# Last down projections of a float32 decoder trunk: loads, high parts, sums and low parts chained in the order of the matmuls; the final gain loaded in four pieces

## The chip, the cores and the metric

The kernel runs on one core of a Trainium2 chip. Its time is the device time of one execution in microseconds; smaller is better. A trace of one profiled execution is read beside it. PE is the matmul engine (PEld its weight loads), DVE the vector engine, ACT the scalar engine, POOL the general-purpose engine, and SP the sequencer that issues nearly all loads.

## What is computed

The reference is a two-layer decoder trunk on 256 tokens of width 2048, all in float32. The first layer has a gated spatial mixer, the second a latent attention; both attend to a memory and end in a gated feed-forward block. The change is in the feed-forward block of the second layer and in the final norm:

```python
def conv_ffn(h, w_up, cw, cb, w_down):
    ...
    gate, val = c[..., :D_FF], c[..., D_FF:]
    return (jax.nn.silu(gate) * val) @ w_down
...
x = x + conv_ffn(rmsnorm(x, g_ffn[l]), w_up[l], conv_w[l], conv_b[l], w_down[l])
return rmsnorm(x, g_final)
```

`w_down` is 5632 x 2048 (44 row blocks of 128).

## The kernel before

**Two parts for each number.** A float32 product is made of three matmuls in the faster type fp32r: every operand is split into a high part (a rounding copy on ACT, tile `whi`) and a low part (the rest, a subtraction on DVE, tile `wlo`), and PE adds high x high, high x low and low x high. So each weight tile of 128x1024 that is loaded (tile `raw` or `gate`) needs one copy on ACT and one subtraction on DVE before PE can use it; the first and third matmul need only `whi`, the second needs `wlo`. There are 4 buffers for `whi`, 5 for `wlo`, 4 for `raw`, 2 for `gate`: a load waits until the subtraction that last read its buffer is done, and a copy into `whi` waits until PE has done with the tile that had the buffer.

**The second layer's feed-forward.** It goes in three parts of 4, 4 and 3 groups of 512 columns (`FF_GROUPS`). In each part PE first makes the hidden values (up projections, L156 to L159, weights through L117 and L118), then the down projection of those columns in two phases, one for each half of 1024 output columns (`down_phase`). A phase walks over blocks `k` of two row blocks each, in an order written out in `FF_FAST`: (0, 1, 2, 5, 3, 6, 7, 4) in the first two parts, with the blocks 2, 3 and 4 "fast"; in the third part (0, 1, 3, 2, 4, 5) with 1 and 2 fast, and then (0, 1, 2, 3, 4, 5) with 1 fast.

A plain block takes its two tiles as they are (`plain_pair`) and costs 24 matmuls of 512 columns, 2 copies and 2 subtractions. A fast block (`fast_pair`) does the 2x2 block product with 7 products in place of 8 (21 matmuls). For that DVE makes four sums of quarter tiles into two tiles `xs` (L720 to L723) from the block's tiles x and y; then y, the two `xs` tiles (L715, L716) and the left half of x (tile `we`, L726, L727) are split. Its products use them in the order y, the second `xs` tile, the first `xs` tile; the product with `we` can stand anywhere. The two tiles of a fast block come into `gate` buffers, except those of the first fast block in a part, which come into `raw`. The same two `gate` buffers hold the up projection's gate values before; the second of them comes free only with the last product "gate times value" (L863, tile `hv`) of the part.

**Who sets the order.** The code is written block after block, but a scheduler that is part of the build orders the instructions of each engine by its own model of their times. It may move a sum, a copy or a load ahead of others that stand before it in the code, and each engine then works strictly in the order that it was given: an instruction that waits holds up all behind it. Only in the last two blocks of the last phase (`late=2`) does the code fix the order for PE, DVE and ACT.

**The end.** `Tokens` collects the results: `between` copies the four extra sums of a phase's fast blocks (tiles `staged`), `combine` folds them into the residual `xt` (six DVE operations, L1353), `evict` adds the four plain sums (L1372) and, in the third part, squares them and multiplies with the final gain `gb` (L1392). `gb` is `g_final` repeated over the 128 partitions, 1 MB as it lands, loaded in one piece at the start of the third part's first phase (L1341).

Of the kernel before, what the change touches and what calls it, by code (L numbers as in the profile page):

```python
# [8 lines left out]
F32 = mybir.dt.float32  # L9
# [3 lines left out]
AF = mybir.ActivationFunctionType  # L13
ALU = mybir.AluOpType
AX = mybir.AxisListType

P = 128
D = 2048
# [55 lines left out]
class Kernel:  # L74
# [235 lines left out]
    def gains(self, names):  # L310
        self.gain_turn(self.gain_load(names, self.nc.sync))
# [352 lines left out]
    def halves(self):  # L664
        tiles = [self.ap.tile([P, NB // 2, 512], F32R, tag=f"xhl{i}", name=self.uid("xhl")) for i in range(2)]
        return [tiles[k // (NB // 2)][:, k % (NB // 2), :] for k in range(NB)]
# [28 lines left out]
                done()  # L695


    def plain_pair(self, raws):
        nc, out = self.nc, []
        for raw in raws:  # L700
            hi, lo = self.split_tile("whi", True), self.split_tile("wlo", True)
            nc.scalar.activation(hi, raw, AF.Copy)
            nc.vector.tensor_tensor(lo, raw, hi.bitcast(F32), ALU.subtract)  # L703
            out.append((hi, lo))
        return out

    def fast_pair(self, raws, pool):
        nc, tt = self.nc, self.nc.vector.tensor_tensor
        left, right = slice(0, 512), slice(512, 1024)
        x, y = raws  # L710
        sums = [self.tmp(pool, [P, 1024], "xs", 2) for _ in range(2)]

        def parts(w):
            hi, lo = self.split_tile("whi", True), self.split_tile("wlo", True)
            nc.scalar.activation(hi, w, AF.Copy)  # L715
            tt(lo, w, hi.bitcast(F32), ALU.subtract)  # L716
            return [(hi[:, c], lo[:, c]) for c in (left, right)]

        t13, t24 = sums
        tt(t13[:, left], x[:, left], x[:, right], ALU.add)  # L720
        tt(t13[:, right], x[:, right], y[:, right], ALU.add)
        tt(t24[:, left], t13[:, left], y[:, right], ALU.add)  # L722
        tt(t24[:, right], t24[:, left], y[:, left], ALU.add)  # L723
        b21, b22 = parts(y)
        one = self.tmp(pool, [P, 1040], "we", 1, F32R)[:, :1024]
        nc.scalar.activation(one[:, left], x[:, left], AF.Copy)  # L726
        tt(one[:, right], x[:, left], one[:, left].bitcast(F32), ALU.subtract)  # L727
        b11 = one[:, left], one[:, right]
        t2, t4 = parts(t24)
        t1, t3 = parts(t13)  # L730
        return b21, b22, t4, t2, t1, t3, b11


    def down_phase(self, dn, col, order, fast, lhs, rhs, pool, fp, between, evict, finish, late=0):
        mm = self.nc.tensor.matmul
        names = ("m1", "m5", "m6", "m7"), ("e00", "e01", "e10", "e11")
        acc = {n: self.psum() for group in names[::-1] for n in group}
        left, right = slice(0, 512), slice(512, 1024)
        todo = {n: 0 for n in acc}
        for k in order:  # L740
            for n in ("m1", "m5", "m6", "m7", "e00", "e01", "e10") if k in fast else names[1]:
                todo[n] += 1 if k in fast else 2
        total = dict(todo)

        def three(n, x, w, out=None, ends=None):
            (xh, xl), (wh, wl) = x, w
# [3 lines left out]
            mm(o, xh, wh, start=start, stop=False)  # L750
            mm(o, xh, wl, start=False, stop=False)  # L751
            mm(o, xl, wh, start=False, stop=stop)  # L752

        def plain(k, ws, tb, half, **kw):
            cols = (left, right)[half]
            for i, (wh, wl) in enumerate(ws):
                three(f"e{tb}{half}", lhs(2 * k + i, tb), (wh[:, cols], wl[:, cols]), **kw)

        kept = []
        last_fast = [k for k in order if k in fast][-1]  # L760
        for n, k in enumerate(order):
            raws = []
            for i in range(2):
                if k in fast and (col or k != fast[0]):
# [3 lines left out]
                self.nc.sync.dma_start(out=raw, in_=dn[(2 * k + i) * P : (2 * k + i + 1) * P, col : col + 1024])  # L768
                raws.append(raw)
            if k in fast:  # L770
                names7 = "e00", "e01", "e10", "m6", "m5", "m7", "m1"
                for name, q, w in zip(names7, (1, 6, 2, 5, 4, 3, 0), self.fast_pair(raws, pool)):
                    three(name, rhs(k, q), w)
                if k == last_fast:
                    between([acc[m] for m in names[0]])
            else:
                ws = self.plain_pair(raws)
                if n < len(order) - late:
                    for tb in range(2):
                        for half in range(2):  # L780
                            plain(k, ws, tb, half)
                else:
                    kept.append((k, ws))
        if not late:
            for tb in range(2):
                for half in range(2):
                    evict(tb, half, acc[f"e{tb}{half}"])
            return
        ET = mybir.EngineType
        with self.tc.manual_schedule(engines={ET.PE, ET.DVE, ET.Activation}):  # L790
            for half in range(2):
                for k, ws in kept:
# [12 lines left out]
            evict(1, 1, e, 0)  # L805
            for i, (wh, wl) in enumerate(ws):
                three("e11", lhs(2 * k + i, 1), (wh[:, 768:], wl[:, 768:]), out=rest[:, 256:], ends=(i == 0, i == 1))
            evict(1, 1, rest, 1)
            finish(1)


    def ffn(self, l, after=None, to_tokens=None, tokens=None):
        nc, t = self.nc, self.t
# [4 lines left out]
        with self.tc.tile_pool(name=self.uid("ff"), bufs=1) as fp:  # L818
            g0 = 0
            for part, ng in enumerate(FF_GROUPS):  # L820
                h = self.ap.tile([P, NB * 512], F32R, tag="big", name=self.uid("h"))
                last = part == len(FF_GROUPS) - 1
                phases = FF_FAST[ng] if tokens is not None else (((), ()), ((), ()))
                fast = phases[0][0]
                if tokens is None:
                    plain = {k: h[:, 1024 * k : 1024 * (k + 1)] for k in range(2 * ng)}
                else:
                    parts7, o = {}, 0
                    for k in fast:
                        n = 896 if k in phases[1][0] else 1024  # L830
# [63 lines left out]
                dn = down[g0 * 512 : (g0 + ng) * 512]  # L894
                g0 += ng
                if tokens is not None:

                    rhs = lambda k, q: tuple(parts7[k][:, i, q * P : (q + 1) * P] for i in range(2))

                    def lhs(k, tb):  # L900
                        if k // 2 in parts7:
                            return rhs(k // 2, ((0, 7), (1, 2))[k % 2][tb])
                        x = block(k)
                        return x[:, tb * P : (tb + 1) * P], x[:, S + tb * P : S + (tb + 1) * P]

                    for ph in range(2):
                        tokens.begin(ph, last)
                        self.down_phase(
                            dn, 1024 * ph, phases[ph][1], phases[ph][0], lhs, rhs, tokens.pool, fp, tokens.between, tokens.evict, tokens.finish, late=2 if last and ph else 0
                        )  # L910
                    continue
                for j in range(4):
# [387 lines left out]
class Tokens:  # L1300
# [32 lines left out]
    def begin(self, ph, last):  # L1333
        k = self.k
        self.ph, self.last = ph, last
        if ph == 0:
            self.staged = k.ap.tile([P, 2, 4, 512], F32, tag="xT", name=k.uid("staged"))
            if last:
                self.gb = k.ap.tile([P, 2 * D], F32, tag="xhl0", name="gb")[:, :D]
                g = k.t["g_final"].rearrange("(o d) -> o d", o=1).to_broadcast([P, D])  # L1340
                self.nc.sync.dma_start(out=self.gb, in_=g)  # L1341

    def between(self, accs):
        for i, acc in enumerate(accs):
# [98 lines left out]
```

## Time and profile before

| what | value |
|---|---|
| device time, 3 runs | median 2054.26 us (2053.43 to 2055.97) |
| profiled execution: its own time, its span | 2056.95 us, 2055.2 us |
| busy share of the span: PE, DVE, ACT, POOL | 99%, 73%, 54%, 7% |
| mean granted clock of PE | 0.998 |
| bytes read from HBM | 387.88 MB, 190 GB/s over the span |
| the chain that ended last | PE 88%, DVE 6%, DMA 4%, issue 1%, ACT 1% |
| loads of `w_ffn_down` into `raw`, into `gate` | 152 and 24 of 512 KB, median 4.6 and 4.8 us from issue to landing |

The span is the stretch from the first to the last instruction; the device time of that execution is 1.75 us longer. A row of a timeline gives the start and the length of an instruction, and in brackets how long its engine stood idle before it and what ended the idle time. Matmuls overlap, so the start of one to the start of the next is what one costs. Lines like L716 are lines of the kernel before.

### The profile page before, as it was taken

What the parts mean: (1) busy time and instruction counts of PE and PEld (TensorE: products, weight loads), DVE (VectorE), ACT (ScalarE), POOL (GpSimd) and SP (SyncE); (2) the same over time, 40 slices, a digit from 0 to 9 for tenths busy, and PEclk for the clock granted to TensorE, in tenths of its full rate; (3) what the DMA queues carried; (4) which work ended last, traced back from release to release, by engine and by line L of the source; (5) the groups of instructions that cost most, each with busy time, mean ns of one, the idle gap of its engine ahead of it and who ended that gap; (6) DMA issues with size and microseconds to landing.
All of it is one profiled execution on the core that took longest, in us unless ns stands there. A gap on an engine that the chain in (4) does not pass through costs nothing.

```text
span 2055.2 us, 39936 instructions
## 1 busy us (share of the span) xinstructions
PE 2034.6 (99%) x16229; PEld 1962.0 (95%) x16229; DVE 1503.4 (73%) x2280; ACT 1114.7 (54%) x1611; POOL 142.0 (7%) x200
## 2 busy tenths in 40 slices
PE   9999999999999999999999999999999999999997
PEld 8889999999999999999999999999988999889976
DVE  6866767767656776567788787777787777878777
ACT  6754744555435554345545675455555555555554
POOL 0000013000000000000042242300000000000000
PEclk9999999999999999999999999999999999999999
DMA  8776566666666666666665535668755766557653
GB/s 251 230 218 181 165 194 194 193 193 193 195 194 194 195 195 195 194 192 192 193 195 183 172 119 165 195 193 228 216 190 179 204 193 206 187 176 205 195 192 135
DMA packets 233821, 394.68 MB, mean 192 GB/s; under 512 B 53854, under 2 KB 61348, under 8 KB 233508
## 3 DMA queue, kind: packets, MB, share of 16 engines
q1 hardware_dynamic: 233444, 391.58, 63.5%
q8 instruction: 127, 2.08, 0.4%
q14 instruction: 58, 0.48, 0.1%
q10 hardware_dynamic: 192, 0.54, 0.1%
HBM read 387.88 MB, written 2.10 MB: 190 GB/s over the span
## 4 chain that ended last, share of the span: by engine, by line
PE 88%; DVE 6%; DMA 4%; issue 1%; ACT 1%; SPq 0%; DVEq 0%; ACTq 0%
PE ps L156 25%; PE ps L157 25%; PE ps L159 25%; DMA gate<-in_w_ffn_down 3%; PE ps L188 2%; PE ps L189 2%; PE ps L190 2%; DVE wlo L703 2%; DMA raw<-in_w_ffn_down 1%; DVE wlo L716 1%; PE ps L523 1%; PE ps L751 1%; PE ps L752 1%; PE ps L750 1%; DVE xs L722 0%
## 5 line engine op out<-in xcount | busy, mean ns | idle before, releaser
L118 DVE TENSOR_TENSOR wlo<-raw,whi 128x1024 fp32r<-128x1024 f32 x572 | 710.1, 1245 | 383.4 <-ACT whi L117 378.7
L117 ACT ACTIVATE whi<-raw 128x1024 fp32r<-128x1024 f32 x572 | 607.1, 1062 | 685.8 <-PE ps L157 583.3
L156 PE MATMUL ps<-xhl,whi 128*128 128x256 f32 x3264 | 762.9, 277 | 0.0
L157 PE MATMUL ps<-xhl,whi 128*128 128x256 f32 x3264 | 761.3, 276 | 0.0
L156 PEld LDWEIGHTS ps<-xhl,whi 128*128 128x128 f32 x3264 | 612.9, 188 | 0.4
L157 PEld LDWEIGHTS ps<-xhl,whi 128*128 128x128 f32 x3264 | 612.7, 188 | 0.4
L159 PE MATMUL ps<-xhl,wlo 128*128 128x256 f32 x3264 | 436.6, 276 | 0.0
L159 PEld LDWEIGHTS ps<-xhl,wlo 128*128 128x128 f32 x3264 | 400.4, 188 | 0.0
L156 PE MATMUL ps<-h,whi 128*128 128x256 f32 x704 | 163.6, 276 | 0.0
L157 PE MATMUL ps<-h,whi 128*128 128x256 f32 x704 | 163.6, 276 | 0.0
L157 PEld LDWEIGHTS ps<-h,whi 128*128 128x128 f32 x704 | 131.9, 188 | 0.0
L156 PEld LDWEIGHTS ps<-h,whi 128*128 128x128 f32 x704 | 131.9, 188 | 0.0
L156 PE MATMUL ps<-mainhl,whi 128*128 128x256 f32 x512 | 119.6, 277 | 0.0
L157 PE MATMUL ps<-mainhl,whi 128*128 128x256 f32 x512 | 119.4, 276 | 0.0
L844 ACT ACTIVATE c<-a,cT 128x256 f32<-128x256 f32 x176 | 99.4, 590 | 10.7 <-DVE a L236 10.6
L157 PEld LDWEIGHTS ps<-mainhl,whi 128*128 128x128 f32 x512 | 96.0, 188 | 0.0
L156 PEld LDWEIGHTS ps<-mainhl,whi 128*128 128x128 f32 x512 | 95.9, 188 | 0.0
L159 PE MATMUL ps<-h,wlo 128*128 128x256 f32 x704 | 94.1, 276 | 0.0
L751 PE MATMUL ps<-wlo,h 128*128 128x512 f32 (+1 forms) x228 | 90.1, 395 | 3.8 <-DVE wlo L716 2.7
L752 PE MATMUL ps<-whi,h 128*128 128x512 f32 (+1 forms) x228 | 88.9, 390 | 0.0
L123 DVE SCALAR_TENSOR_TENSOR wlo<-raw,gT,whi 128x512 fp32r<-128x512 f32 x96 | 72.2, 789 | 22.0 <-ACT whi L122 21.9
L122 ACT ACTIVATE whi<-raw,gT 128x512 fp32r<-128x512 f32 x96 | 63.7, 715 | 43.6 <-PE ps L157 21.5
(376 smaller groups left out, 2729.0 us busy)
## 6 DMA issues: line engine op xcount, KB each, us to landing
raw<-in_w_ffn_up SPq DMA_DIRECT2D x352, 512.0 KB, 4.4
raw<-in_w_ffn_down SPq DMA_DIRECT2D x152, 512.0 KB, 4.6
raw<-in_w_out SPq DMA_DIRECT2D x64, 512.0 KB, 4.7
raw<-in_w_in_a SPq DMA_DIRECT2D x56, 512.0 KB, 4.3
raw<-in_w_mem_kv SPq DMA_DIRECT2D x31, 512.0 KB, 4.6
gate<-in_w_ffn_down SPq DMA_DIRECT2D x24, 512.0 KB, 4.8
raw<-in_w_in_b SPq DMA_DIRECT2D x16, 512.0 KB, 4.5
raw<-in_w_kv_a SPq DMA_DIRECT2D x9, 512.0 KB, 5.4
```

What stands on the lines that cost most here:

```text
L117: nc.scalar.activation(hi[:, :n], raw[:, :n], AF.Copy)
L118: nc.vector.tensor_tensor(lo[:, :n], raw[:, :n], hi[:, :n].bitcast(F32), ALU.subtract)
L122: nc.scalar.activation(hi[:, s], raw[:, s], AF.Copy, scale=gains[k])
L123: nc.vector.scalar_tensor_tensor(lo[:, s], raw[:, s], gains[k], hi[:, s].bitcast(F32), ALU.mult, ALU.subtract)
L156: mm(acc[:, :S], wh, x[:, :S], start=first, stop=False)
L157: mm(acc[:, :S], wh, x[:, S:], start=False, stop=False)
L159: mm(acc[:, :S], wl, x[:, :S], start=False, stop=last)
L188: mm(acc, xh, wh, start=first, stop=False)
L189: mm(acc, xh, wl, start=False, stop=False)
L751: mm(o, xh, wl, start=False, stop=False)
L752: mm(o, xl, wh, start=False, stop=stop)
L844: nc.scalar.activation(c, a, AF.Identity, scale=w(2), bias=w(3))
```

## The change

Three things are changed. A helper `behind` ties an instruction to the one that it last saw on the same engine, so that the scheduler must keep them in the order of the code; it adds no semaphore. With it the loads of the down projections (SP), the copies into `whi` and `we` (ACT), and the sums and subtractions (DVE) of one part stand on their engines in the order of the blocks; other instructions may still come between them. Within a fast block the four sums now stand first in the code, and `we` right behind the parts of y. And `g_final` is loaded in four pieces of 512 columns, one behind the loads of each block from the third on in the third part's first phase.

```diff
+    def behind(self, ins):
+        engine = ins.ins.engine
+        if engine in self.chain:
+            order = mybir.DependencyInfo(mybir.DependencyClass.NoSync, mybir.DependencyReason.DATA)
+            self.tc.add_manual_dep(ins.ins, self.chain[engine], order, reason="behind")
+        self.chain[engine] = ins.ins.name
+        return ins
+
+    def parts(self, w, hi, lo):
+        self.behind(self.nc.scalar.activation(hi, w, AF.Copy))
+        self.behind(self.nc.vector.tensor_tensor(lo, w, hi.bitcast(F32), ALU.subtract))
...
     def fast_pair(self, raws, pool):
...
-        t13, t24 = sums
-        tt(t13[:, left], x[:, left], x[:, right], ALU.add)
...
+        add = lambda o, a, b: self.behind(self.nc.vector.tensor_tensor(o, a, b, ALU.add))
+        add(t13[:, left], x[:, left], x[:, right])
+        add(t13[:, right], x[:, right], y[:, right])
+        add(t24[:, left], t13[:, left], y[:, right])
+        add(t24[:, right], t24[:, left], y[:, left])
...
-                self.nc.sync.dma_start(out=raw, in_=dn[(2 * k + i) * P : (2 * k + i + 1) * P, col : col + 1024])
+                self.behind(self.nc.sync.dma_start(out=raw, in_=dn[(2 * k + i) * P : (2 * k + i + 1) * P, col : col + 1024]))
                 raws.append(raw)
+            if late_gains is not None and 2 <= n:
+                late_gains(n - 2)
...
+                    self.chain = {}
                     for ph in range(2):
...
-                g = k.t["g_final"].rearrange("(o d) -> o d", o=1).to_broadcast([P, D])
-                self.nc.sync.dma_start(out=self.gb, in_=g)
+
+    def gains(self, n):
+        c = slice(512 * n, 512 * (n + 1))
+        g = self.k.t["g_final"].rearrange("(o d) -> o d", o=1)[:, c].to_broadcast([P, 512])
+        self.k.behind(self.nc.sync.dma_start(out=self.gb[:, c], in_=g))
```

In the new kernel L707 is every copy into `whi` and `we`, L708 every such subtraction, L721 every sum, L775 the load of a tile, L1354 that of a piece of the gain. The numbers in the names below tell buffers apart; the second is the scheduler's own.

**DVE, first part, first phase.** 587 and 588 are x and y of the fast block 3, 610 and 611 those of the fast block 4, `raw` 598, 599, 604 and 605 the plain blocks 6 and 7 between them. Before:

```order
L727 TENSOR_TENSOR we_2593_18928<-gate_2587_18914,we_2593_18928 128x512
L721 TENSOR_TENSOR xs_2589_18918<-gate_2587_18914,gate_2588_18916 128x512
L722 TENSOR_TENSOR xs_2590_18919<-xs_2589_18918,gate_2588_18916 128x512
L716 TENSOR_TENSOR wlo_2592_18925<-gate_2588_18916,whi_2591_18924 128x1024
L723 TENSOR_TENSOR xs_2590_18919<-xs_2590_18919,gate_2588_18916 128x512
L716 TENSOR_TENSOR wlo_2595_18932<-xs_2590_18919,whi_2594_18931 128x1024
L716 TENSOR_TENSOR wlo_2597_18936<-xs_2589_18918,whi_2596_18935 128x1024
L720 TENSOR_TENSOR xs_2612_19036<-gate_2610_19032 128x512
L721 TENSOR_TENSOR xs_2612_19036<-gate_2610_19032,gate_2611_19034 128x512
L703 TENSOR_TENSOR wlo_2601_18965<-raw_2598_18960,whi_2600_18964 128x1024
L727 TENSOR_TENSOR we_2616_19046<-gate_2610_19032,we_2616_19046 128x512
L722 TENSOR_TENSOR xs_2613_19037<-xs_2612_19036,gate_2611_19034 128x512
```

and now, from the same place on:

```order
L721 TENSOR_TENSOR xs_2589_18918<-gate_2587_18914,gate_2588_18916 128x512
L721 TENSOR_TENSOR xs_2590_18919<-xs_2589_18918,gate_2588_18916 128x512
L721 TENSOR_TENSOR xs_2590_18919<-xs_2590_18919,gate_2588_18916 128x512
L708 TENSOR_TENSOR wlo_2592_18925<-gate_2588_18916,whi_2591_18924 128x1024
L708 TENSOR_TENSOR we_2593_18928<-gate_2587_18914,we_2593_18928 128x512
L708 TENSOR_TENSOR wlo_2595_18932<-xs_2590_18919,whi_2594_18931 128x1024
L708 TENSOR_TENSOR wlo_2597_18936<-xs_2589_18918,whi_2596_18935 128x1024
L708 TENSOR_TENSOR wlo_2601_18965<-raw_2598_18960,whi_2600_18964 128x1024
L708 TENSOR_TENSOR wlo_2603_18969<-raw_2599_18962,whi_2602_18968 128x1024
L708 TENSOR_TENSOR wlo_2607_19001<-raw_2604_18996,whi_2606_19000 128x1024
L708 TENSOR_TENSOR wlo_2609_19005<-raw_2605_18998,whi_2608_19004 128x1024
L721 TENSOR_TENSOR xs_2612_19036<-gate_2610_19032 128x512
```

The sums for block 4, which stood ahead of the low parts of blocks 6 and 7, stand behind them; the low part of y (`wlo_2592`) now comes behind the fourth sum, and `we_2593`, which was first, behind `wlo_2592`.

**SP, third part, first phase.** `gate` 406 and 407 are x and y of the fast block 2, `raw` 400 and 401 the plain block 3 ahead of it, 417 to 424 the plain blocks 4 and 5 behind it. Before:

```order
L768 DMA raw_3389_24064<-in_w_ffn_down 128x1024
L1341 DMA gb_24018<-in_g_final 128x2048
L768 DMA raw_3390_24066<-in_w_ffn_down 128x1024
L768 DMA raw_3400_24110<-in_w_ffn_down 128x1024
L768 DMA raw_3401_24112<-in_w_ffn_down 128x1024
L768 DMA raw_3417_24196<-in_w_ffn_down 128x1024
L768 DMA raw_3418_24198<-in_w_ffn_down 128x1024
L768 DMA raw_3423_24232<-in_w_ffn_down 128x1024
L768 DMA raw_3424_24234<-in_w_ffn_down 128x1024
L768 DMA gate_3407_24148<-in_w_ffn_down 128x1024
L768 DMA gate_3447_24334<-in_w_ffn_down 128x1024
L768 DMA gate_3448_24336<-in_w_ffn_down 128x1024
```

and now:

```order
L775 DMA raw_3400_24109<-in_w_ffn_down 128x1024
L775 DMA raw_3401_24111<-in_w_ffn_down 128x1024
L1354 DMA gb_24018<-in_g_final 128x512
L775 DMA gate_3406_24146<-in_w_ffn_down 128x1024
L775 DMA gate_3407_24148<-in_w_ffn_down 128x1024
L1354 DMA gb_24018<-in_g_final 128x512
L775 DMA raw_3417_24197<-in_w_ffn_down 128x1024
L775 DMA raw_3418_24199<-in_w_ffn_down 128x1024
L1354 DMA gb_24018<-in_g_final 128x512
L775 DMA raw_3423_24234<-in_w_ffn_down 128x1024
L775 DMA raw_3424_24236<-in_w_ffn_down 128x1024
L1354 DMA gb_24018<-in_g_final 128x512
```

The first tile of the pair was issued at the head of the part (one row above `raw_3383`), the second behind four tiles that PE takes later; now both stand ahead of those four, which wait behind them.

**DVE, third part, where the second phase begins.** `gate` 447 and 448 belong to the fast block 1 of the second phase, `raw` 441 and 442 to its block 0, 417 to 424 to the last two blocks of the first phase. Before:

```order
L720 TENSOR_TENSOR xs_3449_24338<-gate_3447_24334 128x512
L721 TENSOR_TENSOR xs_3449_24338<-gate_3447_24334,gate_3448_24336 128x512
L703 TENSOR_TENSOR wlo_3420_24201<-raw_3417_24196,whi_3419_24200 128x1024
L727 TENSOR_TENSOR we_3453_24348<-gate_3447_24334,we_3453_24348 128x512
L722 TENSOR_TENSOR xs_3450_24339<-xs_3449_24338,gate_3448_24336 128x512
L703 TENSOR_TENSOR wlo_3422_24205<-raw_3418_24198,whi_3421_24204 128x1024
L703 TENSOR_TENSOR wlo_3426_24237<-raw_3423_24232,whi_3425_24236 128x1024
L723 TENSOR_TENSOR xs_3450_24339<-xs_3450_24339,gate_3448_24336 128x512
L703 TENSOR_TENSOR wlo_3428_24241<-raw_3424_24234,whi_3427_24240 128x1024
L703 TENSOR_TENSOR wlo_3444_24303<-raw_3441_24298,whi_3443_24302 128x1024
L703 TENSOR_TENSOR wlo_3446_24307<-raw_3442_24300,whi_3445_24306 128x1024
```

and now:

```order
L708 TENSOR_TENSOR wlo_3420_24203<-raw_3417_24197,whi_3419_24202 128x1024
L708 TENSOR_TENSOR wlo_3422_24207<-raw_3418_24199,whi_3421_24206 128x1024
L708 TENSOR_TENSOR wlo_3426_24240<-raw_3423_24234,whi_3425_24239 128x1024
L708 TENSOR_TENSOR wlo_3428_24244<-raw_3424_24236,whi_3427_24243 128x1024
L708 TENSOR_TENSOR wlo_3444_24306<-raw_3441_24301,whi_3443_24305 128x1024
L708 TENSOR_TENSOR wlo_3446_24310<-raw_3442_24303,whi_3445_24309 128x1024
L721 TENSOR_TENSOR xs_3449_24341<-gate_3447_24337 128x512
L721 TENSOR_TENSOR xs_3449_24341<-gate_3447_24337,gate_3448_24339 128x512
L721 TENSOR_TENSOR xs_3450_24342<-xs_3449_24341,gate_3448_24339 128x512
L1385 TENSOR_TENSOR xt_16474<-ps_3375_24019,xt_16474 128x512
L1366 TENSOR_TENSOR staged_3374_24017<-staged_3374_24017 128x512
L721 TENSOR_TENSOR xs_3450_24342<-xs_3450_24342,gate_3448_24339 128x512
```

The four sums and `we_3453`, which were spread among the low parts of the first phase's last blocks, stand behind those of the second phase's block 0, beside the first additions into `xt` and `staged`.

More of the change, by code (lines that the diff above doesn't have):

```diff
@@ L698, in plain_pair @@
     def plain_pair(self, raws):
-        nc, out = self.nc, []
+        out = []
         for raw in raws:
[L701 to L704, printed above, removed]
+            out.append((self.split_tile("whi", True), self.split_tile("wlo", True)))
+            self.parts(raw, *out[-1])
         return out
     def fast_pair(self, raws, pool):
-        nc, tt = self.nc, self.nc.vector.tensor_tensor
@@ L709, in fast_pair @@
         left, right = slice(0, 512), slice(512, 1024)
         x, y = raws
-        sums = [self.tmp(pool, [P, 1024], "xs", 2) for _ in range(2)]
-        def parts(w):
+        t13, t24 = [self.tmp(pool, [P, 1024], "xs", 2) for _ in range(2)]
+        add = lambda o, a, b: self.behind(self.nc.vector.tensor_tensor(o, a, b, ALU.add))
[3 more added lines that the diff above has]
+        add(t24[:, right], t24[:, left], y[:, left])
@@ L723, in fast_pair @@
[L723 to L724 removed]
+        b21, b22 = halves(y)
         one = self.tmp(pool, [P, 1040], "we", 1, F32R)[:, :1024]
[L726 to L727 removed]
         b11 = one[:, left], one[:, right]
[L729 to L730 removed]
+        self.parts(x[:, left], *b11)
+        t2, t4 = halves(t24)
@@ L731, in fast_pair, with down_phase @@
+        t1, t3 = halves(t13)
         return b21, b22, t4, t2, t1, t3, b11
-    def down_phase(self, dn, col, order, fast, lhs, rhs, pool, fp, between, evict, finish, late=0):
+    def down_phase(self, dn, col, order, fast, lhs, rhs, pool, fp, between, evict, finish, late=0, late_gains=None):
         mm = self.nc.tensor.matmul
@@ L908, in ffn @@
                         self.down_phase(
-                            dn, 1024 * ph, phases[ph][1], phases[ph][0], lhs, rhs, tokens.pool, fp, tokens.between, tokens.evict, tokens.finish, late=2 if last and ph else 0
+                            dn, 1024 * ph, phases[ph][1], phases[ph][0], lhs, rhs, tokens.pool, fp, tokens.between, tokens.evict, tokens.finish, late=2 if last and ph else 0, late_gains=tokens.gains if last and not ph else None
                         )
```

6 lines of the change are left out of this document (2 added, 4 removed).

## The prediction

> **What bounds the kernel now.** I read the page first, then busy time by stretches, then PE's own timeline, and last the chain of waits. The page's first part gives the bound:
>
> ```profile
> PE 2034.6 (99%) x16229; PEld 1962.0 (95%) x16229; DVE 1503.4 (73%) x2280; ACT 1114.7 (54%) x1611; POOL 142.0 (7%) x200
> ```
>
> PE is the bound, so the change can win only what PE loses while it waits in the three stretches of down projections of the second layer. Busy time in these (length; PE, PEld, DVE, ACT, POOL busy; granted clock, DMA share, GB/s):
>
> ```profile
> 1496.42:1581.00 84.58, 82.99 (x362) 67.18 (x361) 69.92 (x91) 46.53 (x55) 0.00 (x0) 1.00 0.54 180
> 1756.80:1842.00 85.20, 83.36 (x362) 67.25 (x361) 69.97 (x92) 46.43 (x56) 0.00 (x0) 1.00 0.54 179
> 1973.63:2046.00 72.37, 66.75 (x287) 52.86 (x285) 61.21 (x90) 39.85 (x61) 0.00 (x0) 0.98 0.38 127
> ```
>
> PE stands idle 1.6, 1.8 and 5.6 us there. The price of a wait is read from starts. First part, first down matmul and the waits, with the idle time in brackets:
>
> ```profile
> 1496.42 0.40 PE L750 MATMUL ps<-whi,h 128*128 128x512 f32 x1
> ...
> 1523.19 0.39 PE L752 MATMUL ps<-whi,h 128*128 128x512 f32 x1
> 1523.76 0.50 PE L751 MATMUL ps<-wlo,hmv 128*128 128x512 f32 x1 [0.18 <-DVE wlo L703]
> 1524.10 0.40 PE L752 MATMUL ps<-whi,hmv 128*128 128x512 f32 x1
> ...
> 1565.16 0.50 PE L751 MATMUL ps<-wlo,h 128*128 128x512 f32 x1 [1.18 <-DVE wlo L716]
> ...
> 1567.50 0.50 PE L751 MATMUL ps<-wlo,hmv 128*128 128x512 f32 x1 [0.22 <-DVE wlo L703]
> ```
>
> The order has 118 matmuls between the first two rows: 26.77 / 118 = 0.227 us each. The step to 1523.76 is 0.57 and the next 0.34, so 0.18 us of idle time costs 0.45: idle time plus 0.27. The three waits cost 0.45 + 1.45 + 0.49 = 2.4 us. The second and third part, by the same rule:
>
> ```profile
> 1784.72 0.50 PE L751 MATMUL ps<-wlo,hmv 128*128 128x512 f32 x1 [0.73 <-DVE wlo L703]
> ...
> 1825.74 0.50 PE L751 MATMUL ps<-wlo,h 128*128 128x512 f32 x1 [0.88 <-DVE wlo L716]
> ...
> 1828.08 0.50 PE L751 MATMUL ps<-wlo,hmv 128*128 128x512 f32 x1 [0.23 <-DVE wlo L703]
> ...
> 1993.70 0.73 PE L750 MATMUL ps<-whi,h 128*128 128x512 f32 x2 [3.56 <-ACT whi L715]
> 1995.07 0.79 PE L751 MATMUL ps<-wlo,h 128*128 128x512 f32 x1 [0.64 <-DVE wlo L716]
> 1995.66 0.63 PE L752 MATMUL ps<-whi,h 128*128 128x512 f32 x1
> ...
> 1998.49 0.40 PE L751 MATMUL ps<-wlo,h 128*128 128x512 f32 x1
> ...
> 2001.56 0.50 PE L751 MATMUL ps<-wlo,h 128*128 128x512 f32 x1 [0.18 <-DVE wlo L703]
> ...
> 2035.57 0.50 PE L751 MATMUL ps<-wlo,h 128*128 128x512 f32 x1 [0.74 <-DVE wlo L703]
> ...
> 2036.70 0.50 PE L751 MATMUL ps<-wlo,h 128*128 128x512 f32 x1 [0.15 <-DVE wlo L703]
> ```
>
> Second part: 1.84 idle + 3 x 0.27 = 2.65. Third: 5.27 + 5 x 0.27 = 6.6, and the 8 matmuls from 1995.66 to 1998.49 take 2.83 in place of 1.81, 1.0 more: 7.6. In all **12.65 us, 0.6%**; more cannot be won here.
>
> **The sums leave the low parts' way: worth 2.4 + 2.65 less what stays.** The chain of waits at the first wait, then the timeline of ACT and DVE at the second:
>
> ```profile
> 1510.34 0.43 DVE hv L863
> 1510.78 3.60 DMA gate<-in_w_ffn_down
> 1515.10 0.60 DVE xs L722
> 1515.70 1.14 DVE wlo L716
> 1517.50 4.35 DMA gate<-in_w_ffn_down
> 1522.49 1.22 DVE wlo L703
> ...
> 1558.18 1.06 ACT L715 ACTIVATE whi<-xs 128x1024 fp32r<-128x1024 f32 x1 [2.35 <-PE ps L752]
> ...
> 1563.28 0.69 DVE L720 TENSOR_TENSOR xs<-gate 128x512 f32<-128x512 f32 x1 [4.63 <-DMA gate<-in_w_ffn_down]
> 1563.88 1.22 DVE L716 TENSOR_TENSOR wlo<-xs,whi 128x1024 fp32r<-128x1024 f32 x1
> ```
>
> In both, DVE is held by a sum for a later fast block whose tile is still on its way, and the low part that PE wants stands behind it: the one of 1563.88 had its high part at 1559.24 and could have run 4.6 us earlier. In the new order (first pair of lists) the sums stand behind these low parts. So all six waits of the two parts go.
>
> What is late next is the second `gate` tile of a part (588). Its load waits for the last `hv`. Ahead of that `hv` the new order has one low part more (1.14) and one sum less (0.60), and earlier on `we` has moved both ways; so it is issued 0.5 to 0.9 later than 1510.78, say at 1511.5, and lands (3.60) near 1515.2. From landing the new order needs 3 sums (1.8), then one copy (1.06) for the high part of the second `xs` tile, 3.0 in all with `we` in between; y's low part is ready after 3.0 too (1.8 + 1.14). PE comes to that `xs` tile at matmul 96, 1496.42 + 96 x 0.227 = 1518.2, and to y's low part at matmul 98, 1518.7. The limit on the landing is thus 1515.2, just met: I leave 0.3 us a part, bounds 0 and 2.0 (below). Gain 2.1 and 2.35.
>
> The loads of raw 598 and 599, which stood ahead of 588, now wait behind it on SP, to about 1512.1 and 1512.7. Their copies come behind those of the fast block, from about 1519.2; even 5.42 us after issue, the slowest gate load quoted below, they are there. That costs nothing; without the fast block's cover it would cost 0.3 to 1 us.
>
> [...]
>
> Whether loads close behind delay 588 is the next question. In the second part two tiles followed 1.1 us behind the same load:
>
> ```profile
> 1771.23 0.33 SPq L768 DMA_DIRECT2D gate<-in_w_ffn_down  x1
> 1772.37 1.80 SPq L768 DMA_DIRECT2D raw<-in_w_ffn_down  x2
> ...
> 1771.23 3.81 DMA gate<-in_w_ffn_down
> ```
>
> It landed after 3.81 all the same, so I take 3.6 to 3.8, though the median of such loads is 4.8:
>
> ```profile
> gate<-in_w_ffn_down SPq DMA_DIRECT2D x24, 512.0 KB, 4.8
> ```
>
> **Third part: the gain and the second tile.** The chain of waits, with the load of the gain from SP's timeline ahead:
>
> ```profile
> 1962.94 0.33 SPq L1341 DMA_DIRECT2D gb<-in_g_final  x1
> ...
> 1964.39 6.84 DMA raw<-in_w_ffn_down
> ...
> 1987.14 5.42 DMA gate<-in_w_ffn_down
> ```
>
> The 1 MB of the gain went out ahead of a tile that then took 6.84 us; without it that tile lands near 1969, and DVE goes on at once. Together with `we` (0.60) leaving the way of the last `hv`, tile 407 is issued about 0.75 earlier, at 1986.4, and lands after 3.7 to 5.4, say 4.3: 1990.7. Its high part is there at 1991.8, where PE has waited since matmul 69, 1973.63 + 69 x 0.227 = 1989.3: 2.5 us in place of 3.56. The `xs` copy is ready at 1993.7; 22 matmuls (5.0) on, with two restarts, PE stands at 1999.2, where it stood at 2001.56 before. Gain 2.4, if PE keeps its clock. The stretch after the long wait and one with a wait of 1.18 (length, PE busy, granted clock, DMA share, GB/s):
>
> ```profile
> 1995.00:1996.00 1.00, 0.93 (x2) 0.50 0.88 340
> 1563.00:1565.20 2.20, 1.02 (x6) 1.00 0.12 47
> ```
>
> After 3.56 us of idle time the clock was 0.50, after 1.18 it was 1.00. A wait of 2.5 lies between, so the 1.0 us of slow matmuls may come back: gain 1.2 to 2.4. [...] Rows alone leave it open; I take the middle, 1.8.
>
> It is not won twice. DVE has no room at the second phase's beginning:
>
> ```profile
> 2008.80:2036.57 27.77, 26.84 (x32) 1.00 0.38 128
> ```
>
> The four sums and `we` (3.0 us) move into this stretch (third pair of lists). It can begin 2.9 earlier, since the loads of block 0's tiles go out with PE's progress, so it ends about where 1.8 to 2.2 are kept, and the two waits at 2035.57 and 2036.70 stay. Third part: 1.8, bounds -0.5 and 3.5.
>
> **Sum.** 2.1 + 2.35 + 1.8 = 6.25. The profiled execution took 2056.95 (span 2055.2); less 6.25, 2050.7. That execution lies 2.7 above the median of the runs, 2054.26, so in these terms **2048.0**. About 0.2%, 4.1 us, is what a measurement of this kernel can tell from no change.
>
> **Rivals.** **B, the wait moves to the second gate tile: no change that can be told.** If loads now packed 0.6 us apart slow it to 5.42 as at 1987.14, it lands at 1516.9 and the `xs` copy comes at 1519.9, 1.7 + 0.27 late in each of two parts: gains 0.4 and 0.65. In the third, with 6.84, it lands at 1993.2, PE goes on at 1994.3, 0.6 later than before: -0.5. Sum 0.55: 2053.7. For it: the median of 4.8, and five tiles and three pieces behind 407. Against: 3.60 and 3.81. Chance 0.26.
>
> **C, slower: sums too late in every fast block.** A fast block costs DVE four sums (2.4), three low parts (3.42) and `we` (0.60), 6.4 us, and PE 21 x 0.227 = 4.77. Before, DVE made sums ahead in idle time; now they stand behind the low parts, and the 1.65 us that DVE lacks may show in each of 15 fast blocks (6 + 6 + 3): 24.7 lost less 12.65 won, 2066.3. It breaks even at 0.84 us a block and is slower by over 0.2% from 1.12. Against it: high parts wait for PE to free a buffer, so DVE idles 14.7 and 15.2 us in the first two stretches, and ahead of the next fast block lie one or two plain ones, in which PE spends 24 x 0.227 = 5.4 and DVE 2.3 each. The last low part waits longest: its high part's buffer comes free 0.7 before the plain block ahead ends, so with 1.06 and 1.14 it is ready 1.5 into the fast block, and PE wants it 18 matmuls, 4.1 us, in. Chance 0.12.
>
> A is my forecast with 0.57; 0.05 is for what I have not seen.
>
> **How the numbers follow.** Faster: A but for its tail under 4.1 (both parts with 1 us left and nothing in the third, gain 3), 0.55, and 0.03 of the rest: 0.58. Same: B and that tail, 0.28. Slower: C and a little of the rest, 0.14. The range runs from nearly all of A's waits gone (10.75 won, 2043.5) past B (2053.7) with its bound of 2 us a part, to 2056.5; C is left out.
>
> **What the new profile would show.** Right: no idle PE at the places of 1565.16 and 1567.50 and of 1825.74 and 1828.08; at the fast block behind 588 under 0.5 us; in the third part one wait of about 2.5 for a high part in place of 3.56, with the clock at 1.00 behind it; the tile of 1964.39 landing in under 5 us. Wrong: PE idle on `wlo<-xs` or `whi<-xs` in most fast blocks (C), or 588 and 407 landing in over 5 us with PE waiting on them (B).

## The result, and the profile after

The changed kernel takes 2052.10 us (median of 20 runs, 2050.82 to 2055.12) where the kernel before, run beside it, takes 2055.33: a ratio of 0.9985, 95% interval 0.9978 to 0.9992. It is 3.2 us faster, 0.15%, in the direction of the forecast and half its size. (One of the 20 runs of the kernel before took 10134.9 us; the ratio leaves it out.) The profiled execution took 2053.55 us (span 2051.8) in place of 2056.95 (2055.2), 3.4 less where the prediction's sum was 6.25. The page's rows on the busy time and on the chain that ended last:

```profile
PE 2034.3 (99%) x16229; PEld 1965.7 (96%) x16229; DVE 1504.8 (73%) x2280; ACT 1113.9 (54%) x1611; POOL 142.5 (7%) x200
...
PE 94%; DVE 3%; ACT 1%; DMA 1%; issue 0%; ACTq 0%
```

PE's share of the chain rose from 88% to 94% and DVE's fell from 6% to 3%. Where the 3.4 us come from is read from the three stretches of down projections, from the first down matmul to the start of the last. Of before:

```profile
1496.42:1582.66 86.24, 84.65 (x371) 68.60 (x370) 71.58 (x93) 48.19 (x57) 0.00 (x0) 1.00 0.53 177
1756.57:1843.24 86.67, 84.83 (x371) 68.52 (x370) 71.44 (x93) 47.90 (x57) 0.00 (x0) 1.00 0.54 176
1973.63:2045.40 71.77, 66.47 (x286) 52.78 (x285) 60.61 (x89) 39.25 (x60) 0.00 (x0) 0.98 0.39 128
```

and after:

```profile
1496.66:1580.99 84.33, 83.58 (x371) 68.93 (x370) 71.92 (x94) 47.64 (x58) 0.00 (x0) 1.00 0.56 187
1754.90:1839.17 84.27, 83.57 (x371) 68.90 (x370) 71.92 (x94) 47.65 (x58) 0.00 (x0) 1.00 0.56 187
1969.56:2042.20 72.64, 67.60 (x286) 54.17 (x285) 60.45 (x89) 38.90 (x60) 0.00 (x0) 0.95 0.41 143
```

The first two parts are 1.91 and 2.40 shorter, the third is 0.87 longer, with a granted clock of 0.95 in place of 0.98. PE's timeline after shows the waits that are left (the middle rows are the second wait of the third part and the first slow matmul behind it):

```profile
1519.36 0.74 PE L757 MATMUL ps<-whi,h 128*128 128x512 f32 x2 [0.75 <-ACT whi L707]
...
1777.54 0.74 PE L757 MATMUL ps<-whi,h 128*128 128x512 f32 x2 [0.70 <-ACT whi L707]
...
1987.85 0.73 PE L757 MATMUL ps<-whi,h 128*128 128x512 f32 x2 [2.47 <-ACT whi L707]
...
1989.93 1.22 PE L757 MATMUL ps<-whi,h 128*128 128x512 f32 x2 [1.05 <-ACT whi L707]
1990.95 0.63 PE L758 MATMUL ps<-wlo,h 128*128 128x512 f32 x1
...
2017.52 0.51 PE L757 MATMUL ps<-whi,h 128*128 128x512 f32 x1 [0.23 <-ACT staged L1358]
...
2033.46 0.51 PE L758 MATMUL ps<-wlo,h 128*128 128x512 f32 x1 [1.28 <-DVE wlo L708]
```

All six waits of before in parts 1 and 2 are gone, and one stands in place of them in each, at the fast block whose second tile waits for the last `hv`. The chain of waits names the tile:

```profile
1511.33 0.35 DVE hv L872
1511.69 4.40 DMA gate<-in_w_ffn_down
...
1516.12 1.31 DVE xs L721 x2
...
1517.45 0.70 DVE xs L721
...
1518.25 1.06 ACT whi L707
...
1519.36 0.74 PE ps L757 x2
...
1769.92 4.35 DMA gate<-in_w_ffn_down
...
1982.38 0.35 DVE hv L872
1982.74 3.92 DMA gate<-in_w_ffn_down
1986.68 1.30 DVE xs L721 x2
1988.01 0.70 DVE xs L721
1988.82 1.06 ACT whi L707
```

The load goes out with the last `hv`, and three sums and a copy stand between its landing and PE. In the third part the same load ends two waits: one of 2.47, which needs only the copy of the tile itself (the high part of y), and one of 1.05, which needs the three sums and the copy. Then the clock is 0.50 for 6.8 us. The rows below (columns as in the prediction) are stretches of 3.41 us, as long as the clock was low before, laid back and forth from the moments at which it changed:

```profile
1985.61:1989.02 3.41, 1.02 (x3) 0.48 (x3) 2.30 (x4) 1.78 (x3) 0.00 (x0) 1.00 0.83 281
1989.02:1992.43 3.41, 2.50 (x6) 2.02 (x7) 3.41 (x4) 2.75 (x3) 0.00 (x0) 0.50 1.02 393
1992.43:1995.85 3.42, 3.42 (x9) 2.65 (x9) 2.65 (x3) 1.54 (x2) 0.00 (x0) 0.50 0.72 264
1995.85:1999.26 3.41, 3.41 (x16) 2.78 (x16) 1.23 (x1) 3.09 (x5) 0.00 (x0) 1.00 0.83 215
```

PE issues 9 matmuls in the third stretch and 16 in the fourth. Before, the clock was low from 1994.71 to 1998.12 only.

### The profile page after: what moved, and what is told of

Its sections match the earlier page's. It is cut to its first block, busy times and chain, and to the rows that moved or that the text cites. A ratio compares the mean times of both kernels' runs of the same rounds, so it can differ in the third digit from the quotient of the medians.

```text
span 2051.8 us, 39921 instructions
## 1 busy us (share of the span) xinstructions
PE 2034.3 (99%) x16229; PEld 1965.7 (96%) x16229; DVE 1504.8 (73%) x2280; ACT 1113.9 (54%) x1611; POOL 142.5 (7%) x200
## 4 chain that ended last, share of the span: by engine, by line
PE 94%; DVE 3%; ACT 1%; DMA 1%; issue 0%; ACTq 0%
PE ps L156 26%; PE ps L157 26%; PE ps L159 26%; PE ps L758 2%; PE ps L759 2%; PE ps L757 2%; PE ps L188 2%; PE ps L189 2%; PE ps L190 2%; DVE wlo L708 1%; PE ps L523 1%; DVE xs L721 1%; DMA gate<-in_w_ffn_down 1%; ACT whi L707 0%; PE ps L603 0%
## 5 line engine op out<-in xcount | busy, mean ns | idle before, releaser
L118 DVE TENSOR_TENSOR wlo<-raw,whi 128x1024 fp32r<-128x1024 f32 x572 | 710.4, 1245 | 385.3 <-ACT whi L117 380.8
L117 ACT ACTIVATE whi<-raw 128x1024 fp32r<-128x1024 f32 x572 | 607.0, 1062 | 687.2 <-PE ps L157 586.6
L708 DVE TENSOR_TENSOR wlo<-raw,whi 128x1024 fp32r<-128x1024 f32 x61 | 73.5, 1222 | 21.8 <-ACT whi L707 21.3
L707 ACT ACTIVATE whi<-raw 128x1024 fp32r<-128x1024 f32 x61 | 64.1, 1057 | 43.8 <-PE ps L759 20.8
```

What stands on the lines that cost most here:

```text
L117: nc.scalar.activation(hi[:, :n], raw[:, :n], AF.Copy)
L118: nc.vector.tensor_tensor(lo[:, :n], raw[:, :n], hi[:, :n].bitcast(F32), ALU.subtract)
L707: self.behind(self.nc.scalar.activation(hi, w, AF.Copy))
L708: self.behind(self.nc.vector.tensor_tensor(lo, w, hi.bitcast(F32), ALU.subtract))
```

## Experiments

Every time stands beside runs of the kernel before on the same chip (medians 2054.32 to 2054.59, and 2055.33 beside the change); the ratio is to these. The last three columns are the lengths of the three parts in the one profiled execution, in us.

| kernel | median us | ratio to before, 95% | part 1 | part 2 | part 3 |
|---|---|---|---|---|---|
| before (3 runs) | 2054.26 | | 86.24 | 86.67 | 71.77 |
| the change | 2052.10 | 0.9985 (0.9978 to 0.9992) | 84.33 | 84.27 | 72.64 |
| the change again | 2051.85 | 0.9987 (0.9978 to 0.9995) | 84.16 | 84.30 | 72.07 |
| pieces alone | 2055.10 | 1.0004 (0.9996 to 1.0013) | 85.36 | 85.39 | 72.55 |
| gain in one piece | 2053.08 | 0.9993 (0.9984 to 1.0003) | 84.16 | 84.22 | 72.21 |
| loads untied | 2053.71 | 1.0001 (0.9992 to 1.0009) | 84.30 | 84.25 | 73.12 |
| ties in parts 1 and 2 | 2051.89 | 0.9986 (0.9977 to 0.9995) | 84.19 | 84.22 | 71.86 |
| y in a raw buffer | 2048.11 | 0.9972 (0.9960 to 0.9984) | 83.25 | 83.24 | 68.12 |
| last fast block untied | 2051.40 | 0.9988 (0.9979 to 0.9997) | 84.14 | 84.20 | 71.26 |
| late combine | 2054.87 | 1.0002 (0.9993 to 1.0010) | 84.25 | 84.28 | 71.35 |
| no first gain | 2052.10 | 0.9989 (0.9980 to 0.9998) | 84.14 | 84.20 | 72.07 |
| all three edits | 2045.39 | 0.9958 (0.9944 to 0.9972) | 83.24 | 83.24 | 64.04 |
| two edits | 2044.60 | 0.9954 (0.9941 to 0.9967) | 83.24 | 83.24 | 65.43 |

**The change again.** No edit.

> The changed kernel a second time, beside the three below. Its time should come out 2.5 to 4 us under the kernel before. The trace tells how much of the third part is chance: if the half clock there (6.8 us long in the first trace, 3.4 in that of the kernel before) follows a window that runs free of the kernel, it may last 3.4 or 6.8 us here, or be missing, with the same waits of about 2.5 and 1.0; if it follows the waits alone, it lasts 6.8 again.

The time repeats. The waits in the third part are 2.52 and 0.43, the low clock again 6.8 us long, but it begins 0.12 ahead of the restart here and 1.17 behind it in the first trace (PE's restart, then the stretches):

```profile
1986.36 1.22 PE L757 MATMUL ps<-whi,h 128*128 128x512 f32 x2 [2.52 <-ACT whi L707]
...
1982.83:1986.24 3.41, 1.01 (x5) 0.51 (x3) 1.05 (x2) 0.99 (x2) 0.00 (x0) 1.00 0.92 236
1986.24:1989.65 3.41, 2.86 (x6) 1.86 (x7) 3.38 (x5) 2.91 (x5) 0.00 (x0) 0.50 0.98 360
1989.65:1993.07 3.42, 3.42 (x10) 2.65 (x9) 3.29 (x4) 2.17 (x3) 0.00 (x0) 0.50 0.85 344
```

So in these two traces the low clock does not begin at a fixed distance from the restart. Of the 13 traces read here ten show it in the third part, two for 3.41 us and eight for 6.83; the other three (y in a raw buffer, all three edits, two edits) have the clock at 1.00 through the part.

**The pieces alone.** Every tie is dropped.

```diff
     def behind(self, ins):
+        return ins
```

> The changed code with no ties at all: PE, DVE and ACT have the order of before, word for word, and SP too, but for the gain in four pieces at the place of the one piece. It is thus the pieces alone. Theory: the same bytes at the same place, so the tile behind them lands as late as before and the time is that of before, within 0.5 us. Rival G (four pieces spread better over the DMA engines): the tile behind lands in under 5 us in place of 6.84, the third part wins 0.5 to 2 us.

PE, DVE and ACT then have the order of before, so the new order of the code within a fast block does nothing by itself, and the four pieces in place of one neither (1.0004, the interval holds 1). This is also a second trace of the order of before, and it says how far one trace can be trusted: its first two parts are 0.9 and 1.3 shorter than in the first. Of the six waits of before, those of 1523.76 and 1784.72 have no like here. The change wins 4.3 in these parts by the one trace and 2.2 by the other.

**The gain in one piece**, at its old place, with all ties; the four late pieces are gone.

```diff
...
+                g = k.t["g_final"].rearrange("(o d) -> o d", o=1).to_broadcast([P, D])
+                self.k.nc.sync.dma_start(out=self.gb, in_=g)
```

> The changed kernel with the gain in one piece at its old place, all ties kept. Theory: the pieces are worth little, since the second tile's load waits for the last hv and not for the gain: 0 to 0.5 us more than the changed kernel. Rival (forecast's step: the tile behind 1 MB lands 2 us late and holds DVE up ahead of the last hv): the wait for the second tile grows by 0.5 to 1.5 us, 2052.5 to 2053.5.

It is 1.0 to 1.2 us above the change, with intervals that overlap, and its waits for the second tile are 2.68 and 0.43. In its trace the tile behind the megabyte takes 6.84 us again, but the second tile goes out only 0.4 us later in the part than in the change (13.6 us after its start, not 13.2). Between nothing and a little over 1 us, the worth of the pieces stays open.

**Loads untied.** The order of DVE, ACT and PE is that of the change, SP's nearly that of before.

```diff
-                self.behind(self.nc.sync.dma_start(out=raw, in_=dn[...]))
+                self.nc.sync.dma_start(out=raw, in_=dn[...])
...
-        self.k.behind(self.nc.sync.dma_start(out=self.gb[:, c], in_=g))
+        self.k.nc.sync.dma_start(out=self.gb[:, c], in_=g)
```

> The changed kernel with the order of DVE, ACT and PE kept, but the loads untied: SP's order is that of before but for three places, and the gain's four pieces stand one behind the other where the one piece stood. If the gain of parts 1 and 2 comes from the order of DVE (theory): both parts keep it (one wait of about 0.7 each), and the third part differs only in its loads, 2051.5 to 2053. Rival L (the order of the loads carries it): waits of before come back in parts 1 and 2, 2054 to 2056.

Parts 1 and 2 keep what they won, so it comes from the order on DVE and ACT. No run tells the two apart; the waits of before were for low parts that stood behind sums on DVE. In the third part the second tile stands behind four tiles that PE takes later, as before, and PE waits longer:

```profile
1988.89 1.22 PE L757 MATMUL ps<-whi,h 128*128 128x512 f32 x2 [3.87 <-ACT whi L707]
```

That is 1.4 over the wait of the change, and the kernel takes 1.6 to 1.9 more, with intervals that just overlap; the third part is 0.5 to 1.05 longer. So the order of the loads seems to earn something, and by the traces in the third part alone. The four pieces moved here too, and one behind the other at the old place they delay the tile behind them again (6.86 us).

**Ties in parts 1 and 2 alone.** The third part has the order of before (the trace is from a second launch of this kernel).

```diff
+        if self.chain is None:
+            return ins
...
-                    self.chain = {}
+                    self.chain = None if last else {}
```

> The changed kernel with the ties in the first two parts alone; in the third, PE, DVE and ACT have the order of before, and SP too but for the gain in four pieces. Theory (the third part's ties lose as much as they win): parts 1 and 2 gain 1.7 and 2.2 against before, the third nothing, about 4 in all: from 1 us less than the changed kernel to the same, between 2050 and 2051.5. Rival (the forecast's third part, 1.8 won there): 1.5 to 2 us more than the changed kernel.

> [...] Theory: parts 1 and 2 show one wait of about 0.7 each, the third the waits of before: 3.6 and 0.6 with slow matmuls behind, 0.2, 0.7 and 0.15.

The time is that of the change to 0.2 us: the third part's ties are worth nothing in sum that the runs can tell. Its waits here are those of before but shorter, 2.79 and 0.48 at the long one, and here the clock was low for 6.8 us, so with this order too it is not always the 3.41 us of before.

**y in a raw buffer.** The second tile of the second fast block no longer waits for the last `hv`.

```diff
+                second = not col and k == fast[1] and i == 1
-                if k in fast and (col or k != fast[0]):
+                if k in fast and (col or k != fast[0]) and not second:
                     raw = self.tmp(fp, [P, 1024], "gate", 2)
```

> The changed kernel, but the second tile (y) of each part's second fast block is loaded into a raw buffer, which comes free long before the last hv. Theory W (what is left in the three parts is the wait for that tile, and the half clock in the third part follows from it): the waits at 1519.36 and 1777.54 go (1.0 us each), in the third part those at 1987.85 and 1989.93 (4.0 with their restarts) and the slow matmuls behind them (2.9): 8.9 us less than the changed kernel, near 2043, granted clock 1.00 all through. Rival O (the wait is the order of sums and copies, not the tile): the xs copies still come late, under 1 us less, near 2051.5. Rival R (each later plain tile gets its raw buffer one tile later): new waits at plain blocks, 2050 to 2054.

4.0 us less than the change (3.7 less than its second launch), not 8.9. Where the tile was, theory W holds to the row: parts 1 and 2 without a wait, the clock at 1.00 throughout.

```profile
1496.36:1579.61 83.25, 83.25 (x372) 69.01 (x370) 72.01 (x94) 47.66 (x58) 0.00 (x0) 1.00 0.55 189
1753.51:1836.75 83.24, 83.24 (x371) 69.00 (x370) 72.01 (x94) 47.66 (x58) 0.00 (x0) 1.00 0.55 190
1967.14:2035.26 68.12, 65.02 (x286) 51.99 (x285) 60.19 (x89) 38.41 (x60) 0.00 (x0) 1.00 0.44 153
```

A part without a wait takes 83.24. In the third part 6.9 us of waits and slow matmuls went and 2.4 came back at the end: PE stands idle 3.1 us there now. PE and DVE's timelines show the longest:

```profile
2026.52 0.50 PE L758 MATMUL ps<-wlo,h 128*128 128x512 f32 x1 [1.91 <-DVE wlo L708]
...
2023.51 1.83 DVE L1367 TENSOR_TENSOR xt<-xt,staged 128x512 f32<-128x512 f32 x2
2025.24 1.22 DVE L708 TENSOR_TENSOR wlo<-raw,whi 128x1024 fp32r<-128x1024 f32 x1
```

PE waits for the last low part, and ahead of it stand two pieces of `combine`. DVE has no idle time from 1998.45 to 2027.5.

**The last fast block untied.** Its loads, sums and `we` may move again.

```diff
-        add = lambda o, a, b: self.behind(self.nc.vector.tensor_tensor(o, a, b, ALU.add))
+        tie = (lambda ins: ins) if free else self.behind
+        add = lambda o, a, b: tie(self.nc.vector.tensor_tensor(o, a, b, ALU.add))
...
-            for name, q, w in zip(names7, (1, 6, 2, 5, 4, 3, 0), self.fast_pair(raws, pool)):
+            for name, q, w in zip(names7, (1, 6, 2, 5, 4, 3, 0), self.fast_pair(raws, pool, free=late)):
```

> The changed kernel, but the loads, sums and the we parts of the last phase's fast block are tied to nothing, so that its sums stand ahead of block 0's low parts again, as before. Theory D (the chain pushed 3.0 us of DVE work into a stretch in which DVE has no idle time, and the waits at 2017.52 and 2033.46 are its price): both waits go or nearly so, 2.0 to 2.4 us less, near 2050. Rival T (the tail's waits come from the additions into xt, which have not moved): they stay, 0 to 0.5 us less.

The wait at 2017.52 goes and the last one shrinks from 1.28 to 0.98: about 1.1 less with their restarts, of 2.0 to 2.4 expected. In medians 0.5 to 0.7, which the intervals don't tell from nothing. By the trace the 3.0 us of sums and `we` are half of what the end of the part loses.

**Late combine.** `combine` of the last phase behind the low parts of the last two blocks.

```diff
-        if self.last and self.ph:
-            self.combine(1)
-        else:
-            self.waiting.append(self.ph)
+        self.waiting.append(self.ph)
...
+        if self.ph and self.waiting and self.last:
+            self.combine(self.waiting.pop())
         add(o, acc[:, c0 : c0 + n])
```

> The changed kernel, but the folding of the last phase's extra sums into xt (combine, 4.6 us of DVE) stands behind the low parts of the last two blocks, not between them. Theory D (DVE without idle time from 2004.8 on is what makes PE wait at 2033.46): that wait goes, the one at 2017.52 stays: 1.4 to 1.6 us less than the changed kernel, provided the last additions bear 4.6 us more ahead of them. Rival E (the wait only moves to the end, where the additions come late): 0 to 0.5 us less.

PE's last wait falls from 1.28 to 0.14, so `combine` ahead of the last low part is what made it, and yet the kernel is 3.0 us slower than the change. DVE's timeline at the end:

```profile
2030.05 1.23 DVE L708 TENSOR_TENSOR wlo<-raw,whi 128x1024 fp32r<-128x1024 f32 x1 [0.81 <-ACT whi L707]
2031.19 1.41 DVE L1363 TENSOR_TENSOR staged<-staged 128x512 f32<-128x512 f32 x2
2032.52 3.68 DVE L1363 TENSOR_TENSOR xt<-xt,staged 128x512 f32<-128x512 f32 x4
2036.12 0.68 DVE L1382 TENSOR_TENSOR xt<-ps,xt 128x512 f32<-128x512 f32 x1
```

The first of the last additions into `xt` now starts at 2036.12, where in the change it starts at 2034.46, though PE there ends 2.2 later. From PE's last matmul to the end it is 13.2 us in place of 9.6. My proviso failed: the end is a chain of DVE and ACT with no room for 4.6 us.

**No first gain.** The four multiplications with `gb` in the last phase's stretch are left out.

```diff
-        if j < 3:
+        if j == 2:
             nc.vector.tensor_tensor(o, o, gb[:, c], ALU.mult)
```

> The changed kernel without the four multiplications with the gain in the last phase's stretch (columns 0 to 1023 are not multiplied by g_final), 2.4 us of DVE less in the tail and nothing else moved but one low part by 0.6. Theory D (DVE without idle time makes PE wait in the tail): the wait of 1.28 goes, the one at 2017.52 shrinks: 1.4 to 2.4 us less than the changed kernel, 2049.5 to 2050.5. Rival H (the last low parts wait for their high parts, which wait for PE): the wait stays, under 0.5 us less.

The wait goes from 1.28 to 1.05, the time stays. So the amount of work on DVE explains little of this wait; the place of `combine` explains most of it, as the run before shows. Theory D holds for what stands ahead of the low part, not for the amount of work.

**All three edits, and two.**

> The changed kernel with all three edits: y of the second fast block in a raw buffer, the last phase's fast block untied, and combine behind the last low parts. Theory (W and D together): no wait on the second tile in any part, clock 1.00 throughout, and the tail's DVE work spread so that its waits shrink from 4.7 us in the first edit alone to under 1.5: 2043, 8 us under the changed kernel (2040.5 to 2046). Rival: the tail is bounded by something else than the place of the DVE work (loads of the last blocks, or DVE's whole work since block 2): the gain stays that of the first edit, 2047 to 2048.

> The kernel with all three edits less the late combine, which made the end 3.5 us later: y of the second fast block in a raw buffer, and the last phase's fast block untied. The end runs from the last matmul in 9.6 us again, as in the changed kernel and in the first edit alone. Theory: PE ends 1 to 1.5 later than with all three (part of the tail's waits come back), the end 3.5 earlier: 2 to 2.5 us under the one with all three, near 2043. Rival (the end was late for another reason): 2045 to 2047.

With all three PE loses 0.7 us in all, but the late `combine` costs its 3.5 at the end. Without it:

```profile
1967.79:2033.22 65.43, 64.13 (x287) 52.30 (x285) 59.92 (x89) 38.76 (x60) 0.00 (x0) 1.00 0.47 158
...
2023.37 0.50 PE L760 MATMUL ps<-wlo,h 128*128 128x512 f32 x1 [1.12 <-DVE wlo L708]
```

The third part is 1.4 longer than with all three (1 to 1.5 expected), and the span 2.6 shorter. 2044.60 us is 0.9954 of before: 7.5 us under the change and the fastest kernel of the study. Both medians are 1.6 to 2.4 above what I expected, though the traces have the waits that I had put down.

## Why the prediction was right, and where it was not

**What bounds it: right.** What the change won, it won from PE's waits: between the two traces the span fell by 3.4 and the three parts by 3.4.

**Sums out of the low parts' way: right.** All six waits went, and 1.91 and 2.40 were won by the traces shown where 2.1 and 2.35 were forecast. Two errors nearly cancel in it, which is luck. The parts lost 3.0 and 3.4 against the 83.24 of a part without waits, not 2.4 and 2.65; and 1.1 and 1.0 are left, not 0.3. The term that was mis-sized is the landing of tile 588: issued at 1511.69, 15.03 after the part's start (15.1 forecast), it took 4.40, in the second part 4.35, where I took 3.6 to 3.8 from two rows of before. Sums and copy then took 3.2 where I had 3.0. Rival B's mechanism, then, at half its price, and the sign of "under 0.5 us" at this block did not come (0.75 and 0.70). Four loads now go out within 1.9 us behind 588, but they alone are not why it takes longer: with the loads untied one follows it by 1.09 us and one goes out 0.38 ahead of it, and it lands about as late, in the first part and in the second:

```profile
1511.43 4.32 DMA gate<-in_w_ffn_down
...
1769.63 4.30 DMA gate<-in_w_ffn_down
```

Before, the nearest load was 1.14 behind it. What lengthens the landing stays open. The median of 4.8 that the prediction set against its 3.6 to 3.8 was no firm ground either: of these 24 loads the trace tells the landing of four.

**Rival C: wrong.** No wait shows in the other fast blocks.

**The third part failed.** Forecast 1.8 won; it is 0.9 and 0.3 longer than before in two traces, and by the medians its ties are worth nothing. The step on the first tile was right: the first fast block's second tile, which went out at 1960.32 now, landed in 3.8 us in place of 6.84.

```profile
raw<-in_w_ffn_down SPq DMA_DIRECT2D x1, 512.0 KB, 3.8
```

PE then waited 2.47 for tile 407 (2.5 forecast), but that number is luck in part: the tile went out 0.3 earlier in its part than before, not 0.75, and landed after 3.92, not 4.3. Two terms behind it were wrong. The first is the clock: I took the middle between 0 and 1.0 us of slow matmuls, and they cost 2.9, since the clock was low for 6.8 us, not for the 3.41 of before; a clock of 1.00 behind the wait had been a sign of being right. No run shows the clock at 1.00 behind a wait for this tile in the third part, on which the upper end of the gain, 2.4, counted: in all ten traces with that wait (about 2.5 to 3.9 us) it was at 0.50, for 3.41 or 6.83 us. The 1.0 itself was misread: before, the 8 matmuls are those from 1995.07 to 1998.49, 3.42 us, so the slow ones had cost 1.6. The second term is the tail. I had the two waits at the end stay at 1.4 with their restarts; with a wait for `staged` and slow starts behind it they are 2.4. The untied block takes 1.1 of this away again, so by the traces the excess comes from the sums and `we`, which the chain pushed there.

**The size.** 1.5 too little left in the first two parts against 1.4 too little counted before, 2.1 to 2.7 too much in the third. The profiled execution should have taken 2050.7 and took 2053.55. That the time lies in the stated range says little, since 2054.26, the time of before, lies in it as well; and the 3.2 us are less than the 4.1 that I took for the least that can be told from no change, though the interval, with 20 runs on each side, leaves 1 out.

## What to carry to other kernels

Ties that keep an engine from waiting for a tile ahead of time paid here, 1.91 and 2.40 us in the first two parts, but what they gave ended at the next late load: look for the buffer that comes free last, and put that tile elsewhere. Here one edit of that kind, with one block let go, took 7.5 us more off, over twice what the ties did. Work moved off one wait lands in another place: ask of both ends, the low part that PE wants next and the chain behind the last matmul, what it now stands ahead of.

## What the runs showed of the hardware

The clock of PE was 0.50 for 3.41 or 6.83 us in the third part of ten traces. The rows of the change and of the change again stand above; these are of the kernel with the pieces alone, then of the kernel before:

```profile
1989.67:1993.08 3.41, 1.51 (x7) 0.93 (x5) 0.00 (x0) 0.00 (x0) 0.00 (x0) 1.00 0.63 222
1993.08:1996.49 3.41, 1.08 (x4) 0.60 (x5) 2.83 (x4) 1.54 (x2) 0.00 (x0) 1.00 0.31 106
1996.49:1999.90 3.41, 3.41 (x9) 2.00 (x8) 2.23 (x3) 3.12 (x4) 0.00 (x0) 0.50 0.55 202
```

```profile
1991.30:1994.71 3.41, 0.73 (x2) 0.30 (x2) 2.12 (x3) 1.54 (x2) 0.00 (x0) 1.00 0.26 74
1994.71:1998.11 3.40, 3.04 (x7) 2.00 (x8) 2.22 (x4) 2.39 (x3) 0.00 (x0) 0.50 0.70 228
```

In the 3.41 us ahead of the low clock PE was busy for 1.02 us (the change), 1.01 (the change again), 1.08 (pieces alone) and 0.73 (before). In the first 3.41 us at 0.50 it was busy for 3.41 (pieces alone) and 3.04 (before), and the clock was 1.00 behind them; for 2.50 (the change), 2.86 (the change again) and 2.93 (ties in parts 1 and 2 alone), and the clock stayed at 0.50 for as long again. What sets the clock was not shown. From start to start, beyond 0.227 us each, the slow matmuls of the third part cost 1.6 us (before, 3.41 us at 0.50) or 2.9 us (after, 6.83 us at 0.50).
